# A hybrid SSD, latent-attention and PEER decoder block: gate stores cut in three, a vector step moved, two loads given to another queue

## The chip, the cores and the metric

The kernel runs on one core of one Trainium2 chip. The core has TensorE (PE, matmuls; PEld is its weight load), VectorE (DVE), ScalarE (ACT), GpSimd (POOL) and SyncE (SP), each with an instruction queue of its own that is worked off in order, and 16 DMA engines that all queues share. DMAs are issued from the SP, ACT and POOL queues here; an issue that has to wait holds up what stands behind it in the same queue. The metric is the device time of one execution in microseconds (us), lower is better.

## The reference, cut to what matters

One layer of a decoder trunk over 512 tokens of width 1024: a mixer (Mamba-2 heads beside latent attention), a layer norm, and then the PEER channel mixer, on which the change lies:

```python
q = (xb @ w_query).reshape(T, PEER_HEADS, 2, PEER_HALF_DIM)
s = jnp.einsum('thkd,hknd->thkn', q, sub_keys)
sv, si = lax.top_k(s, K)                                     # 16 of 128, two halves of 8 heads
cand_s = sv[:, :, 0, :, None] + sv[:, :, 1, None, :]
top_s, top_pos = lax.top_k(cand_s.reshape(T, 8, 256), K)     # 16 of 256
gate = jax.nn.softmax(top_s, axis=-1)
u = jnp.take(u_table, expert_idx, axis=0)
act = jax.nn.gelu(jnp.einsum('td,thkd->thk', xb, u), approximate=False)
v = jnp.take(v_table, expert_idx, axis=0)
return jnp.einsum('thk,thkd->td', gate * act, v)
```

Each token takes 8 x 16 = 128 of 16384 experts. Everything is computed in float32 accuracy.

## The kernel before

Matrix products keep float32 accuracy by splitting each operand into a high and a low part and adding three products (`mm3`, L82, whose three matmuls are L83, L84 and L85). A class `Stream` (L91) brings all weights in chunks of 128x1024: `loads` issues the DMA on SP (L102, tile wir), `his` makes the high part on ACT (L120, tiles wih and wihx), `splits` makes the low part on DVE or POOL (L130, tile wil). So a matmul on a fresh chunk waits for DMA, ACT and DVE in that order.

For PEER the tokens are four blocks of 128. Blocks 0 to 2 (384 tokens) meet the whole expert table densely, except that the last UG = 64 tokens of block 2 have their U side gathered row by row; block 3 is gathered on both sides. The stages around the change are these.

- **U chunks** (`u_half`, `u_chunk`, L1397 to L1417). Each of 128 chunks of 128 experts is multiplied with 320 tokens, 24 matmuls of 128x320 into psum tile pu; ACT puts the GELU of it into an act tile (tiles acts, act; L1408) or, when there is no room, into aout, which SP stores to DRAM (L1411, L1412).
- **`decode`** (L1045) turns the top-16 positions into expert indices and softmax weights (tiles eq, tif, ijg). For blocks 2, 0, 1 it runs ahead of the gates; block 3 runs later, as the first part of the generator `gather` (L1516). After block 2's turn `ug_index` (L1126) starts the gather of U rows for the 64 tokens: POOL fetches a 128x1024 tile urow by an indirect DMA (L1144), DVE forms the dot product with the token tile UR["x"] (L1150), four row buffers. One `next(UR["dots"])` is one such dot; the 65th takes the GELU (L1153), stores it and loads it back transposed as UR["w"] (tile uw, L1154 and L1155, both POOL).
- **`build_g`** (L1215) makes the dense gate matrix of the 384 tokens in 48 steps n of 8 tokens. `hot(n+1)` (L1233) builds one-hot operands on DVE (oj L1238, g L1244), PE multiplies the pair of step n (L1279, L1280, psum tile pw), ACT copies the result into a 2 MB tile stg (L1282; two buffers, used in turn for four steps each). At every fourth step the rows of stg that are not needed on chip go to DRAM by one DMA on ACT's queue (L1290 for the first ten groups; L1292 and L1293 for the two groups of the 64 tokens); two steps later the other rows are multiplied into the activations on chip (L1297). Each step also runs two dots, and steps 36 to 38 run the five parts of `ug_head` (L1160), a chain of small DVE operations that scales uw, ends in a PE transpose (L1174, psum tile px) and puts the result among the gate operands.
- **`drive`** (L1459) interleaves the two lists of work: it keeps a modelled time for PE (`tm[0]`) and one for DVE (`tm[1]`, advanced by what each generator yields) and runs half a U chunk whenever PE's is behind.
- **V chunks** (`v_prep` L1606, `v_hi` L1634, `v_lo` L1640, `v_mm` L1649). The gated activation P (ACT L1617, L1618; or DVE L1614) is split into Ph (ACT L1637) and Pl (DVE L1645) and multiplied with the V rows of chunk c into six psum tiles va (L1654, L1655, L1658). The first two P are made by the loop at L1673; between U chunks that loop and the main loop at L1683 call `pump` (L1316), which runs parts of `gather` for as many modelled microseconds as it is told, and `GS[0]` is -1 until the first of block 3's 256 rows. From then on rows are paced by what is left to do. The P and gt tiles take the memory that the stg tiles leave.

The token tiles UR["x"] and UR["x3"] are loaded by SP (L1494, L1495) into columns of XT that the query projection no longer needs, ahead of iaE (L1501), a constant of `decode`.

Of the kernel before, what the change touches and what calls it, by code (L numbers as in the profile page):

```python
# [31 lines left out]
UG = 64  # L32
NU = NT - UG
ND = NU // 32
FIRST = 44
KEEP = 57
MORE = 12
# [27 lines left out]
def tile_block(ctx: ExitStack, tc: tile.TileContext, I, out):  # L65
    nc = tc.nc
    ctx.enter_context(tc.manual_schedule())
    V, A, T, G = nc.vector, nc.scalar, nc.tensor, nc.gpsimd
# [158 lines left out]
    xsp = dram.tile([NB, 128, D], F32, name="xsp")  # L227
    gs0 = dram.tile([128, 2, UG // 32, 128], F32, name="gs0")
    gsp = dram.tile([NT // 32, 128, 128, 32], F32, name="gsp")
# [459 lines left out]
    for n in range(8):  # L689
# [4 lines left out]
        for kk in range(2):  # L694
            k = kp * 2 + kk
# [249 lines left out]
    wide = lambda z: z.rearrange("p (a b) -> p a b", b=64)  # L945
# [99 lines left out]
    def decode(p, TS, PO, TI, ia, blocks, nb):  # L1045
# [35 lines left out]
        for b in ((2, 0, 1) if nb > 1 else (0,)):  # L1081
            for c in range(2):
                A.activation(ti[:, :, :, :, c].rearrange("p e h a -> p h e a"),
                             TI[:, b].rearrange("p (h e) a -> p h e a", e=2), AF.Copy)
            eq = p.tile([128, 16, 16, 16], F16, name="eq")
            abv = abf[:, b].rearrange("p e (h k) -> p (e h) k", k=16)
            V.tensor_tensor(eq, abv[:, :, None, :].to_broadcast(sh), ia[:, None].to_broadcast(sh), op=OP.is_equal)
            yield 2.3
            eqv = eq.rearrange("p g a (k c) -> p (g a) k c", c=2)
            tv = ti.rearrange("p e h a c -> p (e h a) c")  # L1090
            V.tensor_tensor(eqv, eqv, tv[:, :, None, :].to_broadcast([128, 256, 8, 2]), op=OP.mult)
            if nb > 1 and b == 1:
                yield next(UR["dots"])
            if nb > 1 and b != 1:
                ti = p.tile([128, 2, 8, 16, 2], F16, name="tif", bufs=2)
            yield 2.3
            for w in (8, 4, 2):
                V.tensor_tensor(eq[:, :, :w], eq[:, :, :w], eq[:, :, w:2 * w], op=OP.add)
            V.tensor_tensor(IJG[blocks[b]][:, 0:2].rearrange("p e h k -> p (e h) k"), eq[:, :, 0], eq[:, :, 1], op=OP.add)
            yield 2.8  # L1100
            if nb > 1 and b == 2:
                ug_index(p3)
            if nb > 1 and b == 1:
                yield next(UR["dots"])
                g_head(0)
# [4 lines left out]
    late = []  # L1110
# [12 lines left out]
    GT, UR = {}, {}  # L1123
    done = []
# [90 lines left out]
    def build_g():  # L1215
# [32 lines left out]
                A.activation(g[:, q, :, 8:, c], g[:, q, :, :8, c], AF.Copy, scale=rT[:, m // 2, q, c:c + 1])  # L1248
            return oj, g

        late = []
        digits()
        g_low()
        half(0)
# [2 lines left out]
        dots, head = UR["dots"], ug_head()  # L1257
        tm[1] += 7.5
        yield 2.6
        for n in range(48):  # L1260
            b, g = divmod(n, 16)
# [11 lines left out]
            if g % 4 == 0:  # L1273
                stg = gs[(n // 4 + 1) % 2].tile([128, 128, 32], F32, name="stg")
# [10 lines left out]
            if g % 4 == 3:  # L1285
                k = n // 4
                if k < ND:
                    done.append(min(FIRST, (un[0] - 2) // 4 * 4))
                    late.append((n + 2, k, stg))
                    nc.scalar.dma_start(gsp[k][:, done[k]:], stg[:, done[k]:])  # L1290
                else:
                    nc.scalar.dma_start(gs0[:, :, k - ND], stg[:, 0:8].rearrange("j (q i) t -> j q (i t)", q=2))  # L1292
                    nc.scalar.dma_start(gsp[k][:, 8:], stg[:, 8:])  # L1293
            if late and late[0][0] <= n:
                _, k, z = late.pop(0)
                acts = ALL[0][:, :done[k], k * 32:k * 32 + 32]
# [10 lines left out]
                    lump += 1.1  # L1307
            for _ in range(2):
                tm[1] += next(dots, 0.0)
            for _ in range({36: 2, 37: 2, 38: 1}.get(n, 0)):  # L1310
                tm[1] += next(head)
            yield lump + (1.45 if n + 1 in LOWA else 1.95) if n < 47 else 0.1

# [2 lines left out]
    def pump(g, us):  # L1316
        bal[0] = min(bal[0] + us, us)
        while bal[0] > 0:
            c = next(g, None)
            if c is None:  # L1320
                bal[0] = 0.0
                return False
            bal[0] -= c
        return True
# [31 lines left out]
    aps = [pool("act")]  # L1356
    ALL = [aps[0].tile([128, FIRST, NU], F32, name="acts")]
    out_ = pool("aout")
# [7 lines left out]
    def act_tile():  # L1366
# [5 lines left out]
        an[0] += 1  # L1372
        if n < FIRST:
            return ALL[0][:, n]
        return aps[k].tile([128, NU], F32, name="act", bufs=sizes[k] - (0 if k else FIRST))

    def end_tile():
        while an[0] % LEAD < FIRST:
            an[0] += 1
# [92 lines left out]
    fill = iter(())  # L1472
    for m in range(17):
# [6 lines left out]
        if m:  # L1480
            fill = chain(fill, stage1(m - 1))
# [9 lines left out]
    ug = pool("ug")  # L1491
    UR["x"], UR["x3"] = spare(448), spare(384)
    for i in range(128 // UG):
        nc.sync.dma_start(UR["x"][i * UG:(i + 1) * UG], wide(xsp[2, 128 - UG:]))  # L1494
    nc.sync.dma_start(UR["x3"], wide(xsp[3]))  # L1495
    UR["ix"] = ijp.tile([128, UG], I32, name="uix")
    UR["hd"] = ijp.tile([128, UG], F32, name="uhd")
    UR["g"] = ijp.tile([UG, 128], F32, name="ugw")
# [15 lines left out]
    GS = [-1, 0, 0]  # L1514
# [59 lines left out]
    fill = gather()  # L1574
# [5 lines left out]
    def load_g(q):  # L1580
        if q < 32 and q not in gt:
# [3 lines left out]
            if q < 2:  # L1585
                G.dma_start(gt[q][:, ND:].rearrange("j b i t -> j b (i t)"), gs0[:, q])
            elif nb < ND:
                part(ND, NT // 32)
            if nb:
                part(0, nb if q < 2 or nb < ND else NT // 32)  # L1590

# [81 lines left out]
    for c in range(2):  # L1673
        while uc < PRE - 1 + c:
            u_chunk(uc)
            uc += 1
            pump(fill, 2.6)
        v_hi(c, v_prep(c))
        v_lo()
    more = True  # L1680
# [175 lines left out]
```

## Time and profile before

| what | value |
|---|---|
| median of 3 runs | 1584.36 us (1580.26 to 1591.33) |
| the profiled execution | 1580.1 us |
| its span, first to last instruction | 1578.3 us |
| mean granted TensorE clock | 0.995 |
| PE, DVE, ACT, POOL busy, share of the span | 97%, 86%, 48%, 40% |
| HBM traffic | 411.8 MB, 261 GB/s over the span |

The page gives, for each engine, busy time and share of the span; the windows give the same by stretch, with the granted TensorE clock, the share of time in which the DMA engines were busy, and what they moved. A timeline row gives start, duration, engine, line, operation and, in brackets, how long the engine had idled and what it waited for. Matmuls overlap in the array, so a busy PE can still lose a little between two matmuls; a bracket on PE is time in which it did nothing.

In time the stages stand so: the mixer to about 400 us, query projection and top-16 to about 530, `decode` of blocks 0 to 2 from 531 to 577, `build_g` from there to 846, the first V matmul at 860, the last matmul at 1570, and the last layer norm behind it.

### The profile page before, as it was taken

To read this page: it belongs to the slowest core of one execution; us is meant where nothing else is said; L and a number is where in the kernel's file an instruction comes from. 1 tells how busy PE (TensorE), PEld (TensorE's weight loads), DVE (VectorE), ACT (ScalarE), POOL (GpSimd) and SP (SyncE) were. 2 spreads that over 40 slices of the span, in tenths; PEclk is the share of its full clock that TensorE was granted. 3 is DMA by queue.
4 is the path that set the end of the run, shared out by engine and by line. 5 is a ranking of instruction groups with operands and counts; after the bars stand their busy time and mean duration, and the time that the engine had idled before them with its cause. 6 is when DMAs were issued, how large, how long until landed. Compare 5 with 4: busy or idle time off the path is not lost.

```text
span 1578.3 us, 24433 instructions
## 1 busy us (share of the span) xinstructions
PE 1537.6 (97%) x8696; PEld 1343.0 (85%) x8696; DVE 1357.1 (86%) x2629; ACT 758.9 (48%) x1415; POOL 632.2 (40%) x465
## 2 busy tenths in 40 slices
PE   9999999999999999999998999999999999999997
PEld 7887888888888999998988889989888778888885
DVE  8978767746799998989997788898988899999897
ACT  5565476741433546565666444444443344444342
POOL 0000032500234334434422566565665567656520
PEclk9999999999999999999999999999999999999999
DMA  6242122474323678988977999999999999999983
GB/s 252 94 160 84 52 77 61 124 240 147 124 88 101 149 249 312 338 319 301 389 276 277 329 373 362 367 372 386 375 368 361 371 368 373 387 362 366 342 314 136
DMA packets 152698, 415.48 MB, mean 263 GB/s; under 512 B 18416, under 2 KB 59248, under 8 KB 150784
## 3 DMA queue, kind: packets, MB, share of 16 engines
q1 hardware_dynamic: 98112, 209.68, 38.7%
q0 software_dynamic: 52048, 185.24, 31.5%
q10 hardware_dynamic: 2416, 19.01, 3.0%
q8 instruction: 68, 1.11, 0.3%
q14 instruction: 54, 0.44, 0.1%
HBM read 382.57 MB, written 29.20 MB: 261 GB/s over the span
## 4 chain that ended last, share of the span: by engine, by line
PE 57%; issue 14%; DMA 10%; DVE 10%; POOL 6%; ACT 3%; DVEq 0%; ACTq 0%; SPq 0%; POOLq 0%
PE va L1658 7%; PE va L1655 7%; PE va L1654 7%; POOL row L1537 5%; DMA row<-u,ix 4%; PE pu L83 4%; PE pu L85 4%; PE pu L84 4%; PE pw L84 3%; PE pw L85 3%; PE pa L84 3%; PE pa L85 3%; PE pa L83 3%; PE pw L83 3%; DMA wir<-ut 2%
## 5 line engine op out<-in xcount | busy, mean ns | idle before, releaser
L120 ACT ACTIVATE wih<-wir 128x1024 fp32r<-128x1024 f32 (+2 forms) x269 | 277.8, 1033 | 250.5 <-DMA wir<-ut 101.7
L130 DVE TENSOR_TENSOR wil<-wir,wih 128x1024 fp32r<-128x1024 f32 (+1 forms) x234 | 282.8, 1211 | 59.3 <-ACT wih L120 52.0
L85 PE MATMUL pu<-XT,wil 128*128 128x320 f32 x1008 | 312.1, 310 | 6.6 <-DVE wil L130 6.6
L1655 PE MATMUL va<-wil,Ph 128*128 128x512 f32 x726 | 283.7, 391 | 0.0
L83 PE MATMUL pu<-XT,wih 128*128 128x320 f32 x848 | 265.2, 313 | 4.0 <-ACT acts L1408 1.9
L1537 POOL DMA_INDIRECT row<-v,ix x128 | 210.4, 1644 | 129.9 <-DVE ac L1554 104.9
L84 PE MATMUL pu<-XT,wih 128*128 128x320 f32 x848 | 261.3, 308 | 0.0
L1537 POOL DMA_INDIRECT row<-u,ix x128 | 183.1, 1431 | 120.1 <-DVE row L1548 86.4
L85 PEld LDWEIGHTS pu<-XT,wil 128*128 128x128 f32 x1008 | 189.9, 188 | 9.5 <-DVE wil L130 9.5
L1654 PE MATMUL va<-wih,Ph 128*128 128x512 f32 x474 | 186.0, 392 | 4.4 <-ACT Ph L1637 4.4
L1548 DVE SCALAR_TENSOR_TENSOR row<-row,XT 128x1024 f32<-128x1024 f32 x128 | 150.9, 1219 | 20.7 <-DMA row<-u,ix 20.4
L1554 DVE SCALAR_TENSOR_TENSOR ac<-row,hd,ac 128x1024 f32<-128x1024 f32 x128 | 163.9, 1280 | 4.0 <-DMA row<-v,ix 2.4
L83 PEld LDWEIGHTS pu<-XT,wih 128*128 128x128 f32 x848 | 159.2, 188 | 8.8 <-ACT acts L1408 2.7
L84 PEld LDWEIGHTS pu<-XT,wih 128*128 128x128 f32 x848 | 159.3, 188 | 1.8
L1655 PEld LDWEIGHTS va<-wil,Ph 128*128 128x128 f32 x726 | 136.6, 188 | 27.2 <-DVE wil L130 0.2
L1658 PE MATMUL va<-wih,Pl 128*128 128x512 f32 x474 | 146.8, 391 | 4.0 <-DVE Pl L1645 4.0
L1144 POOL DMA_INDIRECT urow<-u,uix x64 | 99.3, 1551 | 122.0 <-DVE urow L1150 109.3
L130 POOL TENSOR_TENSOR wil<-wir,wih 128x1024 fp32r<-128x1024 f32 (+3 forms) x35 | 73.0, 2093 | 154.9 <-PE pw L85 100.2
L120 ACT ACTIVATE wihx<-wir 128x1024 fp32r<-128x1024 f32 x67 | 71.0, 1060 | 132.9 <-DMA wir<-v 107.7
L1637 ACT ACTIVATE Ph<-P 128x384 fp32r<-128x384 f32 x121 | 62.8, 519 | 106.3 <-DVE P L1614 97.6
L1658 PEld LDWEIGHTS va<-wih,Pl 128*128 128x128 f32 x474 | 89.0, 188 | 24.2 <-DVE Pl L1645 5.3
L1654 PEld LDWEIGHTS va<-wih,Ph 128*128 128x128 f32 x474 | 89.4, 189 | 22.7 <-ACT Ph L1637 4.6
(515 smaller groups left out, 3337.6 us busy)
## 6 DMA issues: line engine op xcount, KB each, us to landing
wir<-ut SPq DMA_DIRECT2D x128, 512.0 KB, 6.2
wir<-v SPq DMA_DIRECT2D x128, 512.0 KB, 7.0
gt<-gsp SPq DMA_DIRECT2D x21, 768.0 KB, 11.0
wir<-wo SPq DMA_DIRECT2D x26, 512.0 KB, 3.6
wir<-wf SPq DMA_DIRECT2D x18, 512.0 KB, 3.2
wir<-wqr SPq DMA_DIRECT2D x16, 512.0 KB, 3.6
gsp<-stg ACTq DMA_DIRECT2D x6, 1344.0 KB, 9.1
de<-acd POOLq DMA_DIRECT2D x8, 512.0 KB, 4.9
```

Source lines behind the costliest of these rows:

```text
L83: T.matmul(ps, lh, rh, start=start, stop=False)
L84: T.matmul(ps, lh, rl, start=False, stop=False)
L85: T.matmul(ps, ll, rh, start=False, stop=stop)
L120: A.activation(h, r, AF.Copy)
L130: self.lo(n).tensor_tensor(l, r, h, op=OP.subtract)
L1144: G.indirect_dma_start(out=UR[n], out_offset=None, in_=I["u"], in_offset=bass.IndirectOffsetOnAxis(ap=UR["ix"][:, n:n + 1], axis=0))
L1537: G.indirect_dma_start(out=R[s], out_offset=None, in_=I["u"] if s < 128 else I["v"], in_offset=bass.IndirectOffsetOnAxis(ap=ix[:, s % 128: ...
L1548: V.scalar_tensor_tensor(wide(r), wide(r), 1.0, x3, op0=OP.mult, op1=OP.mult, accum_out=hd[:, s:s + 1])
L1554: V.scalar_tensor_tensor(ac, r, hd[:, s - 128:s - 127], ac, op0=OP.mult, op1=OP.add)
L1654: T.matmul(va[b][e], Ph[b], h[:, cs], start=c == 0, stop=False)
L1655: T.matmul(va[b][e], Ph[b], l[:, cs], start=False, stop=False)
L1658: T.matmul(va[b][e], Pl[b], h[:, cs], start=False, stop=c == 127)
```

## The change

Five edits. The line numbers of the kernel before are used.

1. The gate rows that went out in one DMA (L1290, L1293) are cut into PIECES = 3 along the expert axis. They stand in a list; each step n issues one, so a group's pieces leave in three steps, and from n = 47 on all that are left.
2. `decode` of blocks 2, 0, 1 no longer runs a dot in the middle of block 1's turn (L1092, L1093). One dot more is then left for `build_g`, which runs it at n = 31, just ahead of the GELU.
3. The five parts of `ug_head` are run as 2, 1, 1, 1 at steps 35 to 38 (they were 2, 2, 1 at 36 to 38).
4. UR["x"] and UR["x3"] are loaded from POOL's queue.
5. The loop that makes the first two P runs `pump` only as long as no row of block 3 has been reached, and with 2.2 us in place of 2.6.

```diff
-            if nb > 1 and b == 1:
-                yield next(UR["dots"])
...
-        late = []
+        late, stores = [], []
...
                     done.append(min(FIRST, (un[0] - 2) // 4 * 4))
                     late.append((n + 2, k, stg))
-                    nc.scalar.dma_start(gsp[k][:, done[k]:], stg[:, done[k]:])
+                    e = [done[k] + (128 - done[k]) * x // PIECES for x in range(PIECES + 1)]
+                    stores.extend((gsp[k][:, x:y], stg[:, x:y]) for x, y in zip(e, e[1:]))
                 else:
                     nc.scalar.dma_start(gs0[:, :, k - ND], stg[:, 0:8].rearrange("j (q i) t -> j q (i t)", q=2))
-                    nc.scalar.dma_start(gsp[k][:, 8:], stg[:, 8:])
+                    e = [8 + 120 * x // PIECES for x in range(PIECES + 1)]
+                    stores.extend((gsp[k][:, x:y], stg[:, x:y]) for x, y in zip(e, e[1:]))
+            while stores:
+                nc.scalar.dma_start(*stores.pop(0))
+                if n < 47:
+                    break
...
-            for _ in range({36: 2, 37: 2, 38: 1}.get(n, 0)):
+            for _ in range({35: 2, 36: 1, 37: 1, 38: 1}.get(n, 0)):
                 tm[1] += next(head)
...
     for i in range(128 // UG):
-        nc.sync.dma_start(UR["x"][i * UG:(i + 1) * UG], wide(xsp[2, 128 - UG:]))
-    nc.sync.dma_start(UR["x3"], wide(xsp[3]))
+        G.dma_start(UR["x"][i * UG:(i + 1) * UG], wide(xsp[2, 128 - UG:]))
+    G.dma_start(UR["x3"], wide(xsp[3]))
...
             u_chunk(uc)
             uc += 1
-            pump(fill, 2.6)
+            if GS[0] < 0:
+                pump(fill, 2.2)
```

On ACT, at the first group of the gate steps (n = 3 and after), before, where one store of 3328 floats a partition stands:

```order
L1282 ACTIVATE stg<-pw 128x128x4 x2
L1290 DMA gsp<-stg 128x3328
L120 ACTIVATE wih<-wir 128x1024
L1408 ACTIVATE acts<-pu 128x320
L1282 ACTIVATE stg<-pw 128x128x4 x2
L120 ACTIVATE wihx<-wir 128x1024
```

and on ACT at the same place in the change:

```order
L1281 ACTIVATE stg<-pw 128x128x4 x2
L1296 DMA gsp<-stg 128x1088
L1413 ACTIVATE acts<-pu 128x320
L121 ACTIVATE wih<-wir 128x1024
L1281 ACTIVATE stg<-pw 128x128x4 x2
L1296 DMA gsp<-stg 128x1120
L1413 ACTIVATE acts<-pu 128x320
L121 ACTIVATE wihx<-wir 128x1024
L1413 ACTIVATE acts<-pu 128x320
L1247 ACTIVATE g<-g,rT 128x16x8 x8
L1281 ACTIVATE stg<-pw 128x128x4 x2
L1296 DMA gsp<-stg 128x1120
```

The same bytes now leave behind three evacuations in place of one, and each of the twelve groups has two issues more.

On DVE, at the end of `ug_head` (uw is the weighted row tile that PE transposes, um its scale), before:

```order
L1168 RECIPROCAL um<-um 64x1
L130 TENSOR_TENSOR wil<-wir,wih 128x1024
L1238 TENSOR_TENSOR oj<-iotaE,jT 128x1024
L1244 TENSOR_TENSOR g<-tens,units 128x64x16
L1297 TENSOR_TENSOR acts<-acts,stg 128x44x32
L1170 TENSOR_SCALAR uw<-uw,um 64x128
L1238 TENSOR_TENSOR oj<-iotaE,jT 128x1024
```

and on DVE at the same place in the change:

```order
L1167 RECIPROCAL um<-um 64x1
L131 TENSOR_TENSOR wil<-wir,wih 128x1024
L1237 TENSOR_TENSOR oj<-iotaE,jT 128x1024
L1243 TENSOR_TENSOR g<-tens,units 128x2048
L1169 TENSOR_SCALAR uw<-uw,um 64x128
L1237 TENSOR_TENSOR oj<-iotaE,jT 128x1024
L1243 TENSOR_TENSOR g<-tens,units 128x64x16
L1302 TENSOR_TENSOR acts<-acts,stg 128x44x32
```

The scaling of uw now stands one step earlier, ahead of the multiplication into the activations, while PE's transpose of it stays in step n = 37.

On DVE, at the first V operands, before:

```order
L1645 TENSOR_TENSOR Pl<-P,Ph 128x384
L130 TENSOR_TENSOR wil<-wir,wih 128x1024
L1091 TENSOR_TENSOR eq<-eq,tif 128x4096
L1098 TENSOR_TENSOR eq<-eq 128x16x128
L1098 TENSOR_TENSOR eq<-eq 128x16x64
L1098 TENSOR_TENSOR eq<-eq 128x16x32
L1099 TENSOR_TENSOR ijg<-eq 128x256
L1645 TENSOR_TENSOR Pl<-P,Ph 128x384
```

and on DVE at the same place in the change:

```order
L1650 TENSOR_TENSOR Pl<-P,Ph 128x384
L131 TENSOR_TENSOR wil<-wir,wih 128x1024
L1092 TENSOR_TENSOR eq<-eq,tif 128x4096
L1650 TENSOR_TENSOR Pl<-P,Ph 128x384
L131 TENSOR_TENSOR wil<-wir,wih 128x1024
L1097 TENSOR_TENSOR eq<-eq 128x16x128
L1097 TENSOR_TENSOR eq<-eq 128x16x64
L1097 TENSOR_TENSOR eq<-eq 128x16x32
L1098 TENSOR_TENSOR ijg<-eq 128x256
```

The second Pl and the next wil now come ahead of the four last additions of block 3's decode.

More of the change, by code (lines that the diff above doesn't have):

```diff
@@ L34 @@
 ND = NU // 32
+PIECES = 3
 FIRST = 44
```

## The prediction, made before the result was known

> **What bounds the kernel now.** I read the page's engine shares first, then the windows over the stretch that the edits touch, then the brackets of PE and DVE in the timeline, then DMA landings. PE is the bound:
>
> ```profile
> PE 1537.6 (97%) x8696; PEld 1343.0 (85%) x8696; DVE 1357.1 (86%) x2629; ACT 758.9 (48%) x1415; POOL 632.2 (40%) x465
> ```
>
> Of a span of 1578.3 us PE idles 40.7, and the change takes no matmul away, so only idle time can be won, and only where the edits lie. The windows of that stretch (us; then PE, PEld, DVE, ACT, POOL busy, granted clock, DMA share, GB/s):
>
> ```profile
> 500.00:550.00 50.00, 50.00 (x322) 48.00 (x321) 48.60 (x250) 23.32 (x34) 19.73 (x11) 1.00 0.57 142
> 600.00:650.00 50.00, 49.94 (x419) 48.65 (x418) 44.38 (x61) 31.28 (x67) 24.20 (x16) 1.00 0.90 328
> 650.00:700.00 50.00, 47.43 (x388) 45.76 (x386) 45.88 (x67) 31.29 (x67) 19.96 (x14) 1.00 0.87 318
> 700.00:750.00 50.00, 47.10 (x369) 45.23 (x368) 45.72 (x61) 31.40 (x68) 23.51 (x16) 0.97 0.88 316
> 750.00:800.00 50.00, 47.93 (x388) 46.46 (x387) 47.34 (x67) 32.42 (x68) 17.20 (x11) 1.00 0.91 337
> 800.00:850.00 50.00, 47.80 (x460) 45.92 (x461) 42.60 (x51) 33.82 (x66) 9.84 (x18) 0.97 0.86 313
> 850.00:900.00 50.00, 45.12 (x230) 39.33 (x229) 38.44 (x60) 25.56 (x49) 22.86 (x25) 0.97 0.81 294
> ```
>
> From 600 to 900 PE idles 0.06 + 2.57 + 2.90 + 2.07 + 2.20 + 4.88 = 14.7 us. That is the purse: 0.9% of the kernel. Seven PE rows hold most of it, with what ended each idle:
>
> ```profile
> 570.87 0.42 PE L85 MATMUL pu<-XT,wil 128*128 128x320 f32 x1 [0.51 <-DVE wil L130]
> 652.16 0.41 PE L83 MATMUL pu<-XT,wih 128*128 128x320 f32 x1 [1.36 <-ACT acts L1408]
> 733.90 0.64 PE L85 MATMUL pu<-XT,wil 128*128 128x320 f32 x1 [2.68 <-DVE wil L130]
> 800.02 0.23 PE L1279 MATMUL pw<-g,oj 128*128 128x128 f16 x1 [1.28 <-DVE g L1244]
> 817.26 0.27 PE L1174 MATMUL px<-ident,uw 64*128 64x64 f32 x1 [2.16 <-DVE uw L1170]
> 859.97 0.80 PE L1654 MATMUL va<-wih,Ph 128*128 128x512 f32 x1 [4.36 <-ACT Ph L1637]
> 867.27 0.50 PE L1658 MATMUL va<-wih,Pl 128*128 128x512 f32 x1 [0.52 <-DVE Pl L1645]
> ```
>
> **Term A, the stores in three pieces.** The waits of 652 and 734 begin with a gate store. Two of them, on ACT, then what ACT and DVE meet:
>
> ```profile
> 638.39 0.33 ACTq L1290 DMA_DIRECT2D gsp<-stg  x1
> 647.10 1.06 ACT L120 ACTIVATE wih<-wir 128x1024 fp32r<-128x1024 f32 x1 [4.69 <-DMA wir<-ut]
> 650.00 1.22 DVE L1150 SCALAR_TENSOR_TENSOR urow<-urow,XT 128x1024 f32<-128x1024 f32 x1 [2.07 <-DMA urow<-u,uix]
> ...
> 719.01 0.33 ACTq L1290 DMA_DIRECT2D gsp<-stg  x1
> 728.95 1.23 DVE L1150 SCALAR_TENSOR_TENSOR urow<-urow,XT 128x1024 f32<-128x1024 f32 x1 [2.16 <-DMA urow<-u,uix]
> 731.47 1.23 DVE L1150 SCALAR_TENSOR_TENSOR urow<-urow,XT 128x1024 f32<-128x1024 f32 x1 [1.29 <-DMA urow<-u,uix]
> ```
>
> The page's DMA issues give the size of most (count, KB each, median us to landing):
>
> ```profile
> gsp<-stg ACTq DMA_DIRECT2D x6, 1344.0 KB, 9.1
> ```
>
> About ten us after the store DVE stands still for a gathered row that has not landed, or ACT for a weight chunk; behind DVE's dot stand wil and g, and PE waits for those. The same comes behind other stores:
>
> ```profile
> 622.85 1.23 DVE L1150 SCALAR_TENSOR_TENSOR urow<-urow,XT 128x1024 f32<-128x1024 f32 x1 [2.73 <-DMA urow<-u,uix]
> 672.84 1.23 DVE L130 TENSOR_TENSOR wil<-wir,wihx 128x1024 fp32r<-128x1024 f32 x1 [1.55 <-ACT wihx L120]
> 694.61 1.23 DVE L130 TENSOR_TENSOR wil<-wir,wih 128x1024 fp32r<-128x1024 f32 x1 [1.59 <-ACT wih L120]
> 788.55 1.23 DVE L130 TENSOR_TENSOR wil<-wir,wih 128x1024 fp32r<-128x1024 f32 x1 [1.90 <-ACT wih L120]
> ```
>
> These seven DVE waits are 13.3 us, in a stretch where DVE is 92% busy, so PE has no way round them. After a long idle the clock is also lower:
>
> ```profile
> 735.00:740.00 5.00, 5.00 (x30) 5.00 (x29) 4.97 (x7) 1.50 (x2) 0.34 (x1) 0.81 0.81 307
> 820.00:825.00 5.00, 5.00 (x47) 4.90 (x45) 4.23 (x8) 3.21 (x6) 0.00 (x0) 0.77 0.87 309
> ```
>
> At 0.81 five us lose 0.95. Between 600 and 800 PE can win at most its idle time there, 7.6, and this 0.95: 8.6. The least is nothing: the bytes are the same and the DMA engines stay about 0.9 busy, so a wait may merely move. Thirds spread over three steps of 4 to 6 us leave the gaps between bursts filled, but not empty engines; I take the middle, **4.3 us won**.
>
> **Term B, the chain.** PE's 2.16 at 817 is a transpose that waits for the scaling of uw, which on DVE stood behind the multiplication into the activations:
>
> ```profile
> 815.40 1.62 DVE L1297 TENSOR_TENSOR acts<-acts,stg 128x1408 f32<-128x1408 f32 x1
> 816.93 0.27 DVE L1170 TENSOR_SCALAR uw<-uw,um 64x128 f32<-64x128 f32 x1
> ...
> 824.78 0.69 DVE L1238 TENSOR_TENSOR oj<-iotaE,jT 128x1024 f16<-128x1024 f16 x1 [0.77 <-PE pw L1280]
> ...
> 841.34 0.69 DVE L1238 TENSOR_TENSOR oj<-iotaE,jT 128x1024 f16<-128x1024 f16 x1 [0.69 <-PE pw L1280]
> ```
>
> In the new order the scaling stands right behind the pair that PE needs for step 37, and 16 gate matmuls lie between, so this wait goes. With the clock behind it (5 x 0.23 = 1.15) it is worth 3.3. But DVE sets the pace here: between 820 and 845 its only idles are those two, 1.5 together, and what DVE has to do stays the same; the next gate step will wait for g. I take **1.5 won**; nothing to 3.3.
>
> **Term C, the first V operands.** PE's 4.36 at 860 ends a chain that starts with the last store:
>
> ```profile
> 846.29 0.62 ACTq L1293 DMA_DIRECT2D gsp<-stg  x1
> 856.08 0.47 ACT L1617 ACTIVATE P<-acts 128x320 f32<-128x320 f32 x1 [0.44 <-DMA gsp<-stg]
> ```
>
> P lies where stg lay, so it waits until the store has read it, 9.8 us. In the change the last group's three pieces leave together behind the same evacuation: same bytes, same landing, so the 4.36 stays (at best it goes whole, at worst the piece left over from the group before adds a third of 9.8, 3.3). The second Pl, in the new order ahead of the four additions, takes away the 0.52 at 867: **0.5 won**.
>
> **Term D, the moved dot.** One dot leaves the decode and comes back at n = 31:
>
> ```profile
> 568.46 1.22 DVE L1150 SCALAR_TENSOR_TENSOR urow<-urow,XT 128x1024 f32<-128x1024 f32 x1
> ```
>
> Its leaving frees DVE ahead of the 0.51 at 571. At n = 31, near 797, it stands ahead of the one-hot pair for which PE waited 1.28 at 800 already, so its 1.2 adds to that. **0.7 lost** (0.5 won to 1.2 lost). Behind the dot, too, wait the GELU, the store and load of uw; the chain starts a step earlier, but the store of uw no longer follows a whole 1.3 MB of gates, so I leave that at nothing.
>
> **Term E, issues.** Two issues more in each of twelve groups, 24 x 0.33 = 7.9 us of ACT's time, on a queue where evacuations of pu, the high parts and the gate copies stand behind each. ACT is busy 31 of 50 us in these windows, and that cover hides most; none (0) and all (7.9) are the ends, **0.5 lost**, nearer the row of cover.
>
> **Term F, loads from POOL.** SP is freed of three issues ahead of iaE, on which DVE waited, and POOL idled:
>
> ```profile
> 541.53 2.29 DVE L1087 TENSOR_TENSOR eq<-abf,iaE 128x4096 f16<-128x4096 f16 x1 [1.13 <-DMA iaE<-ch]
> 552.71 0.56 POOL L1131 DMA_DIRECT2D ugi<-p  x1 [22.25 <-DVE p L1130]
> ```
>
> DVE gains up to 1.1, but PE is busy all of the window 500 to 550, so it is worth **nothing**; the three issues on POOL, 0.56 us each by the row above, lie in its 22 idle us. Uncovered, they would put off the first fetch of rows by 1.7 us. The smaller pump step (2.2 for 2.6) moves block 3's first rows back by one; their pace is set by what is left, so nothing.
>
> **Sum.** 4.3 + 1.5 + 0.5 - 0.7 - 0.5 = 5.1 us won. The profiled execution took 1580.1 us (span 1578.3 and 1.8 around it), so 1575.0; the median of the runs shown is 4.3 above that execution, so about **1579 us**, 0.3% faster. That is less than the 1% that a measurement of this kernel can tell from no change.
>
> **Rivals.** *The thirds change nothing on the DMA side.* The engines are 0.87 to 0.91 busy whichever way the store is cut; then A is 0 and the sum is 0.8 won, **1583.6**. For it speaks that weight chunk and gathered row were late up to ten us after an issue, when the burst is almost over; against it, that the waits follow the stores and not the average. The Trainium skill, DMA: Bandwidth & Descriptors, section "Queues, rings and completion order", has a rule of this kind: each DMA engine goes round the queue rows with work in turn, a packet at a time, so a long store takes its turn and no more. By that rule the cut alone frees nobody while the store lasts, and the time is this rival's; the waits quoted show sharing, and cannot show its turns.
>
> *ACT is the one that pays, and the kernel is slower.* If ACT reaches pieces two and three with evacuations already late, the issues stand on PE's path whole: A gives nothing, B and C 2.0, D takes 0.7, E 7.9: 6.6 lost, **1591**. It decides once ACT has no idle left in the steps with a piece. For it: PE's wait at 652 was for ACT; against: the 18 idle us in each 50.
>
> *All of it comes.* A 8.6, B 3.3, C 0.5, with D and E as above: 11.2 won, **1573**. It needs DVE to be hidden behind PE after 800, where it is not now.
>
> *An edit that does nothing.* If the store of uw is late, the chain at step 35 stalls DVE and B is lost: 1580.5, inside the forecast's own spread.
>
> **How the numbers follow.** Forecast 0.41, first rival 0.30, slower 0.14, all of it 0.13, the rest 0.02. The range reaches from 1569 (all of it, less the scatter of 4 us that the runs show) to 1590 (the first rival plus such a scatter, and most of the slower case). Faster by over 1% means below 1568.5, which needs more than the best case: 0.05. Slower by over 1%, above 1600, needs the slower case and a late last store: 0.03. Within 1%: 0.92.
>
> **What would show it.** Right for A: the seven DVE waits on urow and on ACT's high parts fall from 13 to under 7 us, and PE's idle from 600 to 800 from 7.6 to about 4. For B: no PE idle at L1174's transpose, but one or two of about 1 us on g behind it. For C: the wait of about 4 us on Ph still there, the one on the second Pl gone. For D: a PE wait of about 2 us on g near the 32nd step. For E: ACT's busy share the same and PE waits on acts not more than now. The forecast is wrong if PE's idle from 600 to 900 stays at 14 us or falls below 6, or if the time changes outside 560 to 870.

## The result, and the profile after

The changed kernel took 1578.06 us, median of 20 runs (1571.58 to 1583.78), against 1586.72 us for the kernel before in 20 runs (1578.84 to 1592.79). The ratio is 0.9947 with a 95% interval of 0.993 to 0.9963: 0.53% faster, 8.4 us, between 5.9 and 11.1. The profiled execution took 1575.01 us, with a span of 1573.2 us, 5.1 less than the one before. Single executions of one kernel lie up to 12 to 14 us apart, so in what follows a stage mark of one profile is compared with those of several others.

The engine shares of the changed kernel, on the page:

```profile
PE 1535.1 (98%) x8696; PEld 1343.1 (85%) x8696; DVE 1357.4 (86%) x2629; ACT 756.5 (48%) x1415; POOL 627.6 (40%) x468
```

The number of matmuls is the same and no share moved by more than one point. The windows of the changed kernel over the stretch that the edits touch (us; then PE, PEld, DVE, ACT, POOL busy, clock, DMA share, GB/s):

```profile
600.00:650.00 50.00, 50.00 (x418) 49.18 (x417) 46.03 (x63) 33.56 (x74) 22.28 (x17) 1.00 0.92 334
650.00:700.00 50.00, 48.42 (x390) 47.04 (x390) 48.37 (x71) 31.85 (x69) 24.41 (x16) 0.97 0.92 334
700.00:750.00 50.00, 50.00 (x418) 49.18 (x417) 46.16 (x63) 32.74 (x69) 22.57 (x15) 1.00 0.95 342
750.00:800.00 50.00, 47.26 (x395) 45.85 (x393) 48.16 (x68) 31.01 (x66) 16.26 (x11) 1.00 0.96 339
800.00:850.00 50.00, 48.26 (x455) 46.01 (x453) 39.90 (x49) 33.78 (x66) 9.68 (x18) 1.00 0.88 306
850.00:900.00 50.00, 42.84 (x207) 36.99 (x207) 36.16 (x57) 24.53 (x47) 20.30 (x23) 0.90 0.83 271
```

From 600 to 800 PE idles 0 + 1.58 + 0 + 2.74 = 4.3 us (7.6 before), from 800 to 850 1.7 (2.2 before), but from 850 to 900 7.2 (4.9 before), and the clock there falls to 0.90. From 600 to 900 that is 13.2 us in place of 14.7. The DMA engines move 334 to 342 GB/s where they moved 316 to 337. The rows of PE's timeline after the change, with what ended each idle:

```profile
693.29 0.41 PE L84 MATMUL pu<-XT,wih 128*128 128x320 f32 x1 [1.55 <-ACT act L1413]
795.03 0.23 PE L1278 MATMUL pw<-g,oj 128*128 128x128 f16 x1 [1.14 <-DVE g L1243]
799.05 0.23 PE L1278 MATMUL pw<-g,oj 128*128 128x128 f16 x1 [1.10 <-DVE g L1243]
811.55 0.27 PE L1173 MATMUL px<-ident,uw 64*128 64x64 f32 x1
820.40 0.23 PE L1278 MATMUL pw<-g,oj 128*128 128x128 f16 x1 [1.10 <-DVE g L1243]
859.34 0.79 PE L1659 MATMUL va<-wih,Ph 128*128 128x512 f32 x1 [7.16 <-ACT Ph L1642]
```

The wait of 2.7 us on wil is gone, and so are the one at the transpose and the one at the second Pl. Three waits of 1.1 us on g stand around the 32nd and the 38th step, and the wait of the first V matmul is longer, 7.16 in place of 4.36. Ahead of the gates, at 584.5, PE waits 2.65 us on wil; from 550 to 600 it idled 0.86 in all before. No run was made for this wait.

How DVE's waits changed is told by two groups. For the gathered rows between 600 and 800 us, the view of the tile urow says who waited for it (us, times) and how long a row's load took to land; of the kernel before:

```profile
  DVE urow L1150: 8.3, 4
DMA to landing us min/median/max: 4.7/7.7/13.1
```

and of the changed kernel:

```profile
  DVE urow L1149: 2.0, 2
DMA to landing us min/median/max: 4.9/8.6/11.6
```

The median row lands later than before, the latest one sooner. DVE waits only for the late ones. For the tile wil, DVE's waits until the high part is there (us, times), in the changed kernel:

```profile
  ACT wih L121: 4.6, 4
  ACT wihx L121: 3.2, 2
```

The same two rows of the kernel before:

```profile
  ACT wih L120: 4.9, 4
  ACT wihx L120: 2.4, 2
```

7.8 us against 7.3: these waits did not fall. Of these two groups only the waits of the dots became shorter.

The end of the gates in the changed kernel, in the timeline of ACT, POOL and SP:

```profile
842.81 3.09 ACTq L1296 DMA_DIRECT2D gsp<-stg  x3
...
853.49 0.47 ACT L1622 ACTIVATE P<-acts 128x320 f32<-128x320 f32 x1 [1.35 <-DMA gsp<-stg]
854.02 1.06 POOL L1591 DMA_DIRECT2D gt<-gs  x2 [8.18 <-ACT P L1622]
854.08 0.33 SPq L103 DMA_DIRECT2D wir<-v  x1
858.47 0.26 ACT L1623 ACTIVATE P<-gt 128x64 f32<-128x64 f32 x1 [4.51 <-DMA gt<-gs]
```

and the same load of gt before:

```profile
856.61 1.08 POOL L1586 DMA_DIRECT2D gt<-gs  x2 [9.05 <-ACT P L1617]
...
857.34 0.33 SPq L102 DMA_DIRECT2D wir<-v  x1
...
859.11 0.26 ACT L1618 ACTIVATE P<-gt 128x64 f32<-128x64 f32 x1 [2.56 <-DMA gt<-gs]
```

P starts 2.6 us earlier than before. Its second part waits 4.5 us for the gates' rows gt, before 2.6, and starts only 0.6 us earlier. A weight load of SP, which before was issued 0.7 us after the load of gt, now goes out at the same moment; that this is what makes gt late was not tried.

### The profile page after: what moved, and what is told of

It reads as the page before. It is cut to its first block, busy times and chain, and to the rows that moved or that the text cites. A ratio compares the mean times of both kernels' runs of the same rounds, so it can differ in the third digit from the quotient of the medians.

```text
span 1573.2 us, 24481 instructions
## 1 busy us (share of the span) xinstructions
PE 1535.1 (98%) x8696; PEld 1343.1 (85%) x8696; DVE 1357.4 (86%) x2629; ACT 756.5 (48%) x1415; POOL 627.6 (40%) x468
## 4 chain that ended last, share of the span: by engine, by line
PE 60%; DVE 17%; DMA 9%; issue 7%; ACT 3%; POOL 3%; ACTq 0%; DVEq 0%; POOLq 0%
PE va L1659 8%; PE va L1660 8%; PE va L1663 8%; PE pu L84 6%; PE pu L86 6%; PE pu L85 6%; PE pa L85 3%; PE pa L84 3%; PE pa L86 3%; POOL row L1542 3%; DMA row<-v,ix 2%; DMA row<-u,ix 2%; DMA wir<-v 1%; DVE t L1017 1%; DVE wil L131 1%
## 5 line engine op out<-in xcount | busy, mean ns | idle before, releaser
L1542 POOL DMA_INDIRECT row<-u,ix x128 | 177.9, 1390 | 124.6 <-DVE row L1553 94.8
```

The lines of the kernel that those rows point to most:

```text
L1542: G.indirect_dma_start(out=R[s], out_offset=None, in_=I["u"] if s < 128 else I["v"], in_offset=bass.IndirectOffsetOnAxis(ap=ix[:, s % 128: ...
```

## The experiments

Twelve kernels were timed, each in 12 runs (one in 6) against the kernel before on the same chip, whose median was 1585.75, 1587.12 and 1585.96 us in the three sittings. A ratio is known to about 0.0023, 3.6 us, so small effects stay open. All profiles are put side by side at the end of this section.

**The pieces alone.** The kernel before with edit 1 only.

```diff
-                    nc.scalar.dma_start(gsp[k][:, done[k]:], stg[:, done[k]:])
+                    e = [done[k] + (128 - done[k]) * x // PIECES for x in range(PIECES + 1)]
+                    stores.extend((gsp[k][:, x:y], stg[:, x:y]) for x, y in zip(e, e[1:]))
...
+            while stores:
+                nc.scalar.dma_start(*stores.pop(0))
+                if n < 47:
+                    break
```

> The kernel before with the gate stores in three pieces and nothing else of the change. If the late landings behind the whole stores are what holds DVE and PE (my theory), PE's idle from 600 to 800 us falls from 7.6 to about 4 us, the last evacuation of the gate steps ends 3 to 5 us earlier than the 845.7 of before, and the time is 4 to 5 us lower, ratio about 0.997. If the thirds change nothing on the DMA side (first rival), PE's idle stays at 7 to 8 us and the ratio is 1.000. If ACT pays for 24 more issues, the ratio is 1.002 to 1.005.

1578.53 us; ratio 0.9955 (0.9932 to 0.9977), 7.2 us faster, from 3.6 to 10.8. The windows of this kernel:

```profile
600.00:800.00 200.00, 196.16 (x1612) 190.92 (x1612) 190.03 (x262) 131.25 (x281) 88.92 (x57) 1.00 0.93 335
800.00:850.00 50.00, 47.80 (x462) 46.12 (x460) 39.20 (x48) 31.89 (x63) 9.86 (x18) 1.00 0.90 315
```

PE idles 3.8 us from 600 to 800, 7.6 before, and the last evacuation ends 4.6 us earlier, both as expected; the gain is larger than the 4 to 5 us expected, which its interval still holds. The pieces carry the whole of the change's gain, within the intervals.

**The chain alone.** The kernel before with edit 3 only.

```diff
-            for _ in range({36: 2, 37: 2, 38: 1}.get(n, 0)):
+            for _ in range({35: 2, 36: 1, 37: 1, 38: 1}.get(n, 0)):
```

> The kernel before with the five parts of the small chain spread over steps 35 to 38 and nothing else. My theory: the PE wait of 2.16 us on the scaling of uw goes, about 1.5 us of it comes through to the last evacuation of the gate steps, ratio 0.999. If DVE takes all of it back, 1.000; if the load of uw is late for step 35, DVE idles 1 to 2 us on it and the ratio is 1.001.

1586.67 us; ratio 0.9983 (0.9959 to 1.0008). PE's wait at the transpose is gone, and behind its place stands, in PE's timeline of this kernel:

```profile
826.49 0.23 PE L1279 MATMUL pw<-g,oj 128*128 128x128 f16 x1 [1.18 <-DVE g L1244]
```

Ahead of the chain, at 802.34, PE waits 2.07 us on g, where before it waited 1.28 at 800.02. The last evacuation of the gates ended at 845.8 us, before at 845.7. In this profile DVE takes back what the chain gave.

**The smaller pump alone.** The kernel before with edit 5 only.

```diff
-            pump(fill, 2.6)
+            if GS[0] < 0:
+                pump(fill, 2.2)
```

> The kernel before with only the last edit: the loop that makes the first two P runs smaller parts of the fourth block's decode, 2.2 for 2.6 us, and stops at its first row. My theory: only the PE wait of 0.52 us at the second Pl goes, ratio 0.9995 and no change behind 870 us. The rival that the two traces raise: the order of the fourth block's rows against the V chunks moves as well, PE idle between 1150 and 1300 us falls from 7.9 to about 5.5 us, and the ratio is 0.997 to 0.998.

1585.20 us; ratio 1.0001 (0.9977 to 1.0026). The wait of 0.52 on the second Pl is gone; the time does not show it. The rival's sign came as well: PE idles 5.4 us from 1150 to 1300 where it idled 7.9. But its ratio of 0.997 to 0.998 did not come in the mean, and over the kernels with the same chunks ahead of V this window idles anywhere from 4.8 to 9.6 us.

**The moved dot alone.** The kernel before with edit 2 only.

```diff
-            if nb > 1 and b == 1:
-                yield next(UR["dots"])
```

> The kernel before with the moved dot alone (the last block's decode no longer takes a dot product ahead of its own work). Prediction's term D: 0.7 us lost, so +0.5 to +1.2 us, which a measurement hardly tells from nothing. Rival, from the run with the pieces whole, which was 4.5 us slower than before: the moved dot is what costs there, because one more dot with its gathered row falls among the late gate steps; then this run is 3 to 5 us slower than before.

1587.47 us; ratio 1.0015 (0.9989 to 1.004), 2.4 us slower in the mean with nothing in the interval. The 3 to 5 us of the rival lie in the interval too, so it stays open between them.

**Chain and dot together.** The kernel before with edits 2 and 3.

```diff
-            if nb > 1 and b == 1:
-                yield next(UR["dots"])
...
-            for _ in range({36: 2, 37: 2, 38: 1}.get(n, 0)):
+            for _ in range({35: 2, 36: 1, 37: 1, 38: 1}.get(n, 0)):
```

> The kernel before with the spread chain and the moved dot, stores whole. Theory 'interaction' (with whole stores the dots and the small uw load land late, and the two edits together move the transpose chain onto them): 3 to 5 us slower than before, with a wait of over 1 us on the uw load at the scaling and PE idle in 795 to 850 above the 5 us of before's stretch. Rival 'nothing together' (chain alone -2.7 in the mean with an interval that holds 0, dot alone 0.7 lost): within 2 us of before.

1587.51 us; ratio 1.0009 (0.9988 to 1.003): within 2 us of before in the mean, as the second theory had it, but the interval reaches 4.8 us slower and does not exclude the first. The wait on the load of uw is there as the first had it. DVE's timeline:

```profile
812.38 0.28 DVE L1161 TENSOR_TENSOR uw<-uw,ugw 64x128 f32<-64x128 f32 x1 [1.00 <-DMA uw<-ugh]
```

**The change with whole stores.** The changed kernel with the three pieces undone.

```diff
-PIECES = 3
+PIECES = 1
```

> The changed kernel with its stores whole again (one piece), all other edits kept. By my theory the pieces are the larger half of the gain: the ratio to the kernel before is 0.997 to 0.998, against 0.9947 for the whole change, and the seven long waits of DVE behind the stores are back, about 13 us together. By the first rival it stays at 0.995, the whole gain coming from the other edits.

1589.24 us; ratio 1.0028 (1.0006 to 1.0051), slower than before by 4.5 us (0.9 to 8.1). Neither ratio that was expected came: the pieces are more than the larger half of the gain, and the other edits without them cost time. In the changed kernel, then, the pieces are worth 1.0028 - 0.9947 = 0.0081, 12.8 us, give or take 4.4 (the two intervals together), more than alone. Here too DVE waits for uw, as the prediction's last rival feared:

```profile
816.87 0.28 DVE L1162 TENSOR_TENSOR uw<-uw,ugw 64x128 f32<-64x128 f32 x1 [1.51 <-DMA uw<-ugh]
```

In the changed kernel, with the pieces, nothing waited for that load; nor did anything with whole stores and the chain alone, so it takes the moved dot as well. This run and the one before it overlap in their intervals, so which of edits 2 to 5 costs without the pieces is not settled.

**The pieces in one burst.** The pieces alone, all three issued in the step in which the whole store was.

```diff
             while stores:
                 nc.scalar.dma_start(*stores.pop(0))
-                if n < 47:
-                    break
```

> The kernel before with the gate stores in three pieces, all three issued one after another in the step where the whole store was issued, so that the bytes go out at the same time as before and only their cut is new. Theory 'spread in time' (loads on the other queues waited behind one large store; the pieces help because the bytes come over three steps): the gain of the pieces alone, 7.2 us, is mostly lost; time against before -2 to +1 us, the waits of DVE on urow stay near 2 to 2.7 us each, 13 us or more in the gates. Rival 'smaller DMAs' (each DMA is completed on its own, or takes turns with others more often, whenever it is issued): the gain stays, -6 to -8 us against before, and the longest wait on urow is below 1.7 us.

1582.89 us; ratio 0.998 (0.9957 to 1.0002): 3.2 us faster in the mean, between the theories. The interval reaches from 6.8 us faster to 0.3 slower, so the time is told neither from that of before nor from that of the spread pieces. The trace says more. Who waited for the tile urow from 600 to 800, in this kernel:

```profile
  DVE urow L1151: 4.1, 5
```

Half of before's 8.3, and nearly as little as with the pieces spread (3.6); the longest is 1.60 us, as the rival had it. So the cut alone shortens the waits on rows. But DVE's waits for the tile wil, until ACT's high part is there, in this kernel:

```profile
  ACT wih L121: 9.4, 4
...
  ACT wihx L121: 0.9, 1
```

10.3 us in place of 7.3. The view of the tile wir puts it down to issuing (ACT's idle time ahead of its high parts in which it waited for nothing the profile shows):

```profile
  issue: 11.8, 6
```

Before, no such row stands there. From 611 to 840 us three issues in a row hold ACT 1.5 to 2.5 us in its timeline. The gate steps, from the first evacuation to the last, are as long as before: 255.1 us, before 254.9. This is the rival "ACT pays", in the one form in which it happened, read from one profile: the cut makes the waits on rows shorter, and spreading it over the steps keeps the issues under ACT's idle time.

Why the cut frees the rows is read in the DMA queues of 600 to 800 us (packets, MB, share of 16 engines; q0 carries POOL's gathered rows, q1 SP's weight chunks, q10 ACT's gate stores). Before:

```profile
q0 software_dynamic: 8064, 29.36, 41.2%
q1 hardware_dynamic: 7947, 24.89, 34.4%
q10 hardware_dynamic: 1009, 10.43, 12.7%
```

and with the burst:

```profile
q10 hardware_dynamic: 3024, 10.42, 13.1%
```

The same bytes at the same moment, but a packet of the store has 10.43 MB / 1009 = 10.3 kB before and 3.4 kB with the burst; the rows' have 3.6 kB and the chunks' 3.1 kB (all means over a queue). The Trainium skill (DMA: Bandwidth & Descriptors, section "Queues, rings and completion order") says that an engine goes round the queues with work, one packet at a time. If a packet that the profile counts is such a turn, which no run shows, the whole store took three times its neighbours' bytes in each turn, and the third takes about as much as they do. The queues agree with it while one store is out. Before, from 722 to 727 us:

```profile
q10 hardware_dynamic: 113, 1.20, 57.1%
...
q0 software_dynamic: 72, 0.28, 14.8%
```

and with the burst, from 722 to 729 us:

```profile
q10 hardware_dynamic: 348, 1.13, 39.9%
q0 software_dynamic: 259, 0.96, 34.6%
```

The store takes less of the 16 engines' time and the rows more. At the store of 638 us it is the same: from 641 on the store has 61.5% before and 51.2% with the burst, the rows 12.6% and 28.9%. Packet size by itself, with nothing else changed, was not tried: the burst also has three DMAs in place of one.

**Three rows in flight.** The kernel before with one gathered row less ahead of the dots.

```diff
-UROWS = 4
+UROWS = 3
```

> The kernel before with three gathered rows in flight ahead of the dots in place of four (UROWS 3). Theory 'rows' (a store of 1.4 MB makes the row loads land late, DVE's dots wait for them, the gates wait for DVE, and this is what the pieces take away): with one dot's time less of lead the waits on urow grow from 8 us to over 20 us in the gates and the time by 5 us or more (ratio above 1.003). Rival 'not rows' (the pieces help through something else, the weights' rounding or the evictions on ACT): the waits grow but lie under PE's U work, and the time stays within 2 us of before.

1592.83 us; ratio 1.0036 (1.0013 to 1.0059), 5.7 us slower, as the theory had it. Who waited for urow in it:

```profile
  DVE urow L1150: 22.6, 18
```

14.3 us more of waiting on rows cost 5.7 us of time and put the last evacuation of the gates 9.6 us later: DVE's waits for rows are on the path, though not with their whole length.

**Three rows with the pieces.**

```diff
-UROWS = 4
+UROWS = 3
...
+PIECES = 3
```

> The pieces alone, with three rows in flight in place of four. Theory 'rows': the pieces make a row land sooner, so the loss from the shorter lead is smaller than with whole stores: the gain of the pieces against the same kernel with whole stores (the run before this one) grows to 8 us or more. Rival 'not rows': the two differ by 7 us as with four rows, or less.

1587.26 us; ratio 1.0006 (0.9981 to 1.0031). Against the run with whole stores that is 0.003, 4.8 us, give or take 5.4: the 8 us expected did not come. The number is the rival's, but its reason, that rows do not matter, fell with the run before; what was wrong in the theory is that it took every row to land sooner. Who waited for urow:

```profile
  DVE urow L1151: 21.2, 14
```

With three rows in flight the pieces hardly help the rows (22.6 with whole stores). The landings fit this: a dot comes every 200 / 58 = 3.45 us and takes 1.2, and a row's buffer is free when its dot has ended, so four rows give some 4 x 3.45 - 1.2 = 12.6 us from issue to use and three some 9.1 (estimates from means). The latest rows, up to 13.1 us, are what four miss, and those the pieces bring to 11.6. Later than 9.1 us came 16 of the 54 rows of before whose landing the trace tells, and 14 of 49 in the changed kernel; later than 10.5 us came 10 and 1. The landings of the kernels with three rows are not in their traces, so this stays an argument.

**The stores twice.** The kernel before with the first ten gate stores issued a second time, to a tensor that nothing reads.

```diff
                     nc.scalar.dma_start(gsp[k][:, done[k]:], stg[:, done[k]:])
+                    nc.scalar.dma_start(gsd[k][:, done[k]:], stg[:, done[k]:])
```

> The kernel before with each of the first ten gate stores issued twice, the second time to a DRAM tensor of its own that nothing reads (14 MB more written over 210 us). Theory 'traffic of the stores on the path': what the pieces take away is the time that others wait while a store is out, so twice the store costs 5 us or more, with waits on urow of 3 to 5 us each. Rival 'transfers are hidden': the queues have room (DMA share 0.87 to 0.91 there), and the time stays within 2 us.

1607.06 us in 6 runs; ratio 1.0135 (1.0098 to 1.0172), 21 us slower. Its windows:

```profile
600.00:800.00 200.00, 184.75 (x1441) 175.87 (x1440) 171.93 (x239) 113.72 (x244) 79.45 (x55) 0.97 0.94 358
800.00:850.00 50.00, 42.59 (x364) 39.94 (x363) 39.83 (x51) 32.11 (x68) 8.50 (x15) 0.93 0.85 308
```

PE idles 15.3 us where it idled 7.6, the waits on rows are 17.4 us in twelve times, the longest 3.25 (3 to 5 each was expected), and the clock is lower. No evacuation into stg waited for a store, so it is not the buffers that cost. The store's traffic is on the path; a DMA share of 0.89 was no sign of room.

**Four pieces.** The changed kernel, with a piece in every step.

```diff
-PIECES = 3
+PIECES = 4
```

> The changed kernel with four pieces in place of three, so that a piece goes out in every step of a group. Theory 'spread in time': a little more of the same, 0 to 3 us faster than the changed kernel (ratio to before 0.993 to 0.995), waits on urow below 1 us each. Rival 'ACT pays': one more issue per group on ACT and 5900 packets growing to some 7000, no gain or up to 3 us slower than the changed kernel.

1579.02 us; ratio 0.9962 (0.9938 to 0.9985). Not told from three pieces, 2.4 us worse in the mean. One wait on a row was 2.07 us, so "below 1 us each" was wrong.

**Two more U chunks ahead of V.** The changed kernel, made to fill the 7.16 us wait.

```diff
-PRE = 80
+PRE = 82
...
-RES = 3
+RES = 5
```

> The changed kernel with two more U chunks computed after the gates and ahead of the first V chunk (PRE 82 for 80, RES 5 for 3: the stretch before stays as it is, 24 matmul groups of about 3.5 us a chunk are added between the last gate step and the first V chunk, and taken from the interleaved stretch behind it). Theory: the wait of 7.2 us of the first V matmul on Ph is time lost, because the last gate store lands 11 us after the last eviction while only 10 us of U work stand there; with 17 us of it the wait falls under 1 us and the time by 4 to 7 us against the changed kernel (ratio to before about 0.991). Rival: the wait is given back later (the V chunks that then run without a U chunk between them wait on weights, or DVE and ACT fall behind), so the time stays within 1.5 us of the changed kernel.

1577.69 us; ratio 0.9939 (0.9917 to 0.9962), 0.0008 or 1.3 us under the changed kernel's, which the intervals do not tell from nothing. It is the best mean of all, but no version was shown to beat the changed kernel. The wait went whole. PE's timeline:

```profile
861.62 0.40 PE L1659 MATMUL va<-wih,Ph 128*128 128x512 f32 x1
```

But the time followed by 1.3 us, give or take 4.4, where 4 to 7 were expected; that is less than the 7.2 us filled, and the rival's 1.5 fits. The windows of this kernel behind that place:

```profile
900.00:1150.00 250.00, 246.42 (x1348) 221.09 (x1347) 214.97 (x328) 104.00 (x188) 154.17 (x108) 1.00 0.98 366
1150.00:1300.00 150.00, 140.43 (x697) 120.07 (x696) 135.55 (x158) 57.19 (x101) 88.64 (x61) 0.98 1.00 371
```

and of the changed kernel:

```profile
900.00:1150.00 250.00, 250.00 (x1378) 225.60 (x1377) 220.26 (x335) 106.22 (x193) 154.47 (x111) 1.00 0.99 373
1150.00:1300.00 150.00, 144.46 (x726) 123.70 (x725) 137.31 (x159) 57.90 (x102) 91.41 (x62) 1.00 1.00 376
```

3.6 and 4.0 us more of idle PE: in this pair the 7.2 won ahead of V are given back behind it. One pair does not show it, since the same two windows idle 0 to 6.4 and 4.8 to 9.6 us in the other kernels. The DMA engines stand at 0.98 to 1.00 there in both; that the weights of that stretch cannot come sooner fits it, but was not tried.

Side by side, from each kernel's profile: DVE's waits on rows from 600 to 800, the length of the gate steps from the first evacuation to the end of the last, that end, the first V matmul, and the ratio. The column of waits separates cut stores from whole ones without an overlap, as long as four rows are in flight.

| kernel | waits on rows, us | gate steps, us | last evacuation | first V | ratio to before |
|---|---|---|---|---|---|
| before | 8.3 | 254.9 | 845.7 | 860.0 | 1 |
| chain alone | 9.4 | 254.1 | 845.8 | 859.6 | 0.9983 |
| pump alone | 9.9 | 257.9 | 849.1 | 863.2 | 1.0001 |
| dot alone | 8.6 | 256.7 | 847.6 | 862.3 | 1.0015 |
| chain and dot | 7.4 | 258.1 | 848.3 | 864.2 | 1.0009 |
| change, whole stores | 10.2 | 261.9 | 852.8 | 868.0 | 1.0028 |
| pieces in one burst | 4.1 | 255.1 | 846.9 | 862.3 | 0.998 |
| pieces alone | 3.6 | 247.8 | 841.1 | 856.0 | 0.9955 |
| the change | 2.0 | 248.7 | 842.2 | 859.3 | 0.9947 |
| four pieces | 3.5 | 250.9 | 842.9 | 857.9 | 0.9962 |
| two more U chunks | 3.9 | 250.2 | 841.1 | 861.6 | 0.9939 |
| three rows | 22.6 | 264.9 | 855.3 | 870.3 | 1.0036 |
| three rows, pieces | 21.2 | 265.4 | 855.6 | 869.6 | 1.0006 |
| stores twice | 17.4 | 276.6 | 867.9 | 882.9 | 1.0135 |

The six kernels with whole stores and four rows wait 9.0 us in the mean, need 257.3 for the gate steps and end them at 848.2; the four with spread pieces wait 3.3, need 249.4 and end them at 841.8. The gates end 6.4 us sooner, and the ratios of the four lie 6 to 10 us under before. With DVE's waits on wil counted in, the six wait 15.6 to 19.0 us, the four 9.1 to 11.9 and the burst 14.4: it is both kinds together that go with the length of the gate steps.

The pair of profiles of before and after shows only 3.5 of the 6.4 us at the last evacuation: its gate steps are 6.2 us shorter, but begin 2.8 later, behind the wait at 584.5. At the first V matmul the three spread kernels with the same chunks ahead of it stand at 857.7 in the mean and the six at 862.9. That is 5 us; where the rest of the measured gain lies these profiles do not tell.

## Why the prediction was right, and where it was not

The class, the sign and the place were right: within 1%, a little faster, by shorter waits for late loads while the gates run. The time, 1578.06 for 1579.0, is close by luck: the gain was 8.4 us and not 5.1, and the median of before lay 2.4 us above the one shown, so two misses nearly cancel. The prediction also held that under 1% cannot be told from no change; twenty runs of each told 0.53%, with an interval from 0.37 to 0.70.

**Term A was mis-sized.** The step that failed is "I take the middle", 4.3 us. Measured with its issues in it (A less E, forecast 3.8) it is 7.2 us alone, from 3.6 to 10.8, so that 3.8 is just inside; inside the whole change it is 12.8, give or take 4.4, and 3.8 is outside. The middle was taken because the bytes are the same and the DMA engines were 0.9 busy, so that a wait "may merely move". The bytes stayed and the DMA share rose (0.89 to 0.94), but the latest rows came sooner, and the waits for them fell to about a third (9.0 to 3.3, by the means above). The prediction had also put the waits for ACT's high parts among the seven; they did not move (7.3 and 7.8), so its sign "from 13 to under 7" did not come out: all waits of both kinds are 9.8 us, 15.6 before. PE's idle of "about 4" did, with 4.3. Its sign of being wrong, idle from 600 to 900 that "stays at 14 us", was only just missed: 13.2, of which the wait on Ph is 7.16. Nor do the pieces leave in "three steps of 4 to 6 us": in the first seven groups ACT issued the second piece 0.6 to 3.1 us after the first and the third 6.3 to 8.6 us after the second, one group at 692.42, 693.01 and 699.59.

**The rival of no change on the DMA side** is refuted by the pieces alone, whose interval ends at 0.9977. It was supported with the rule of turns of the Trainium skill, and there the prediction left something out: it took a turn to be equal for all, while the store's packets were three times as long as the others' and the cut makes them about equal.

**Term B** (1.5): the wait at the transpose went and waits of 1.1 us on g came, as forecast. Alone, the chain ends the gates no sooner; its time, 2.7 us faster with an interval from 6.5 faster to 1.3 slower, neither shows nor excludes 1.5. Its rival, uw late, came true only where the stores were whole and the dot moved.

**Term C**: the second Pl's wait is gone, and 0.5 us is under what a run can tell. The wait on Ph did not stay at 4.36 but grew to 7.16, near the bound of the "worst". The reason given for that bound, a piece left over from the group before, isn't what is seen. PE came to the place 3.4 us sooner (852.2 for 855.6), while P began 2.6 and, behind the later load of gt, its second part only 0.6 us sooner. The other two spread kernels with the same chunks wait 5.07 and 5.08 there and those with whole stores 3.88 to 5.91, so part of the 7.16 belongs to this execution. And the wait is not worth its length: without it the time is not told from the same.

**Term D** (0.7 lost): PE waits 1.14 and 1.10 on g around the 32nd step, 2.2 together, where it waited 1.28; about 2 us was forecast. Alone, the dot cost 2.4 us, give or take 4. The 0.51 at 571 is gone, but the 2.65 at 584.5 was not foreseen.

**Term E** (0.5 lost): ACT's share stayed 48%, and PE's waits for an activation from 600 to 800 are not more than before: 2.1 us in two times, before 3.6 in six. The burst shows what the cover is for: without the spreading DVE waits 10.3 us on ACT's high parts.

**Term F**: no run tells it apart; DVE's busy time from 500 to 550 rose by 1.1 us and PE stayed at 50.00.

The prediction also called itself wrong if the time changed outside 560 to 870. In the profiled pair 4.5 of the 5.1 us lie behind the first V matmul. Over all the kernels the time from that matmul to the end runs from 714 to 728 us with no order in the edits (716.3 with whole stores in the changed kernel, 717.0 with the pieces alone), so this looks like the scatter of single executions, and one pair could not have decided that sign.

## What to carry to other kernels

Where an engine waits for small loads, look at the latest landings and at how many are in flight, not at the median or the mean DMA share: here the median row came later and the kernel was faster. A long store beside such loads was worth cutting into thirds, whose packets are about as long as theirs, with the pieces issued where the issuing engine has idle time; fourths were not told from thirds. A wait of PE that is filled is not yet time won: 7 us filled here brought no gain that the runs can tell.

## What the runs showed of the hardware

- One DMA of the gate store went out in packets of 10.3 kB in the mean (600 to 800 us), its thirds in packets of 3.4 kB. From the fifth group to the tenth a store has 84 columns of 128 bytes, 10752 bytes in a row, and a third of it 3584. More packets cost the engines nothing that shows. ACT's queue on the page (packets, MB, share of 16 engines), before:

```profile
q10 hardware_dynamic: 2416, 19.01, 3.0%
```

and after the change:

```profile
q10 hardware_dynamic: 5872, 19.01, 3.0%
```

- An issue on ACT's queue was dearer in a burst. The view by line gives min/median/max in ns; with spread pieces (the change):

```profile
L1296 ACTq DMA_DIRECT2D gsp<-stg x36: 326/326/1474, 612.7 to 845.0; - x36
```

and with the pieces in one burst:

```profile
L1298 ACTq DMA_DIRECT2D gsp<-stg x36: 326/459/1854, 611.2 to 849.9; - x36
```

- 14 MB more of writing over 210 us raised the traffic from 325 to 358 GB/s at a DMA share of 0.94, and cost 21 us.
